# Two column tiles of the last stage made side by side

## The chip, the cores and the metric

The kernel runs on one core of a Trainium2 chip. The metric is device time in microseconds (us) of one execution. Its engines run side by side and meet only through waits: TensorE (PE, with PEld for its weight loads), VectorE (DVE), ScalarE (ACT), GpSimd (POOL) and SyncE (SP), which issues every DMA of the last stage. Each engine takes its instructions strictly in the order in which the program lists them, so that an instruction that waits holds back all that stand behind it on its engine.

## The reference

One layer of a diffusion backbone over 2048 latent tokens and 256 context tokens, width 1024. What matters here is its end, cut down:

```python
b0 = pool_o * silu(pieces[1])
b1 = diff_o * silu(pieces[5])
b2 = gqa_o * silu(pieces[9])
g0, g1, g2 = split(sigmoid(pieces[10]), 3)
y = g0 * (b0 @ w_branch[0]) + g1 * (b1 @ w_branch[1]) + g2 * (b2 @ w_branch[2])
x_new = x + gate * (y @ w_out)
```

`b0`, `b1` and `b2` are 2048 x 512, `w_branch` is three times 512 x 1024, `w_out` 1024 x 1024.

## The kernel before

Before the last stage come the projections, the attention and the gates; none of that is touched. The last stage works on four chunks of 512 tokens, held transposed (128 channels on partitions, 512 tokens in the free dimension). For each chunk it makes eight tiles of `y` (`merge`, phase "m", called m0 to m7 below) and then eight tiles of the output (`finish`, phase "o", called o0 to o7). The 64 steps stand in the list `seq`, in this order, and `n` is a step's place in it.

Products are made in three passes. Each float32 operand is split into a rounded high part and the rest, its low part (`split`: ACT writes the high part, then DVE subtracts it from the source to get the low part), and a product is high x high, high x low, low x high (`PASSES`). A tile of the output is thus 8 tiles of `y` (index k) x 3 passes = 24 matmuls 128x128 by 128x512. Its first two need only the high part of the weights `wt`, the third needs the low part.

What each step of `finish` issues: after k = 3 the split of the `y` tile that was merged last (`late`, set by m7 and therefore only there in o0), the split of the next step's weights (`w_split(n + 1)`), the load of the weights of step n + 3 (`w_load`, 512 KB for an output tile), and the load of the next step's piece of x (`x_load`, the tile `res`); at the end DVE multiplies the sum by the gate and adds x (L1237), and the tile is written out. There are two buffers for raw weights (`wr`) and two for split weights (`wt`): a split of weights can start when the step two before it has done its last matmul, and a load of raw weights when the split of the step two before it is done.

Beside this run the parts of the next chunk's branches: twelve generators (pool g0 to g3, diff h0 to h3, gqa h0 to h3, called p, d and g below), of which `tick`, called once at the head of every step, starts one and takes every active one a stage further. A diff part first issues three loads (L1064: `oD`, `rD`, `sgD`), a tick later multiplies on DVE (L1157, name `b`) and on POOL (L1159, name `b1g`), and a tick later splits the result into `bt` (L1056 on ACT, L1057 on DVE). A pool part makes its `pl` on POOL and DVE (L1131), splits it, and a tick later multiplies it on PE (L1145, `mix`), then on DVE (L1147), and splits it into `bt`. During o0 of the first three chunks the tick starts d1, lets d0 multiply, and lets p3 make `pl`; at o1 it starts d2, lets d1 multiply, and splits p3 and d0; at o2 it starts d3, lets d2 multiply, and splits d1. The last chunk has no parts to make.

All of this is issued in the order in which the Python code is run, on every engine: no scheduler moves it.

Of the kernel before, what the change touches and what calls it, by code (L numbers as in the profile page):

```python
# [16 lines left out]
ALU = mybir.AluOpType  # L17
# [4 lines left out]
P = 128  # L22
D = 1024
KT = D // P
# [14 lines left out]
CH = 512  # L39
# [18 lines left out]
def block_kernel(ctx: ExitStack, tc, x, xT, ctxt, cc, ada_w, ada_bT, norm_gT, w_qkv, w_gate, gains,  # L58
                 rope_row, rope_col, lam, sublnT, pool_w, pool_scaleT, pool_edge, w_br, w_out, out,
                 dbg=None, stop=9):  # L60
    nc = tc.nc
    dma = nc.sync.dma_start
# [26 lines left out]
    gateT = cst.tile([P, KT], F32, name="gateT")  # L89
# [8 lines left out]
    def dump():  # L98
        if dbg:
            for nm, t in (("kD0", kD[0]), ("kD4", kD[4]), ("qD1", qD[1]), ("qD5", qD[5]), ("vD", vD), ("gvD", gvD),  # L100
                          ("oD1", oD[1]), ("oD5", oD[5]), ("uD1", uD[1]), ("sgD1", sgD[1]),
                          ("tD3", tD[3]), ("msD1", msD[1]), ("rD1", rD[1])):
                if nm in dbg:
                    dma(out=dbg[nm], in_=t)
# [12 lines left out]
    def s8(name, shape, dt):  # L117
        return shp.tile(shape, dt, name=name, tag="s8", bufs=8)

    def raw(name):  # L120
        return shp.tile([P, 512], F32, name=name, tag="raw", bufs=4)
# [90 lines left out]
    with tc.tile_pool(name="p1", bufs=1) as sp, tc.tile_pool(name="p1s", bufs=1, space=PSUM) as pp:  # L212
# [242 lines left out]
        wraws, weights, wundo, weps = {}, {}, {}, {}  # L455

        def w_load(kind, k):
            off, width = QKV_CHUNKS[kind]
            wr = sp.tile([P, 512], F32, name="wraw", tag="wraw", bufs=8)
            dma(out=wr[:, :width], in_=w_qkv[k * P:(k + 1) * P, off:off + width])  # L460
            wraws.setdefault(kind, []).append(wr)
# [211 lines left out]
        for n, kind in enumerate(QKV_ORDER):  # L673
# [9 lines left out]
            for t in range(first, NT):  # L683
# [34 lines left out]
                if gating and u < 10:  # L718

                    for m in (2 * u - 4, 2 * u - 3):  # L720
                        if 0 <= m:
                            part, wr = gacc[:, (m % 2) * 512:(m % 2 + 1) * 512], ada_raws.pop(0)
                            if m < 2:
                                nc.vector.tensor_scalar(out=part, in0=wr, scalar1=cct[:, 0, 0:1], scalar2=None,
                                                        op0=ALU.mult)
                            else:
                                nc.vector.scalar_tensor_tensor(out=part, in0=wr, scalar=cct[:, m // 2, 0:1], in1=part,
                                                               op0=ALU.mult, op1=ALU.add)
# [36 lines left out]
    with tc.tile_pool(name="p2", bufs=1) as sp, tc.tile_pool(name="p2s", bufs=1, space=PSUM) as pp:  # L765
# [4 lines left out]
        for n in range(32):  # L770
            for o in range(2):
                rows += [("d", n // 8, n % 8, o, c) for c in range(2)]
                m = 2 * n + o
# [233 lines left out]
        for i in range(NR + 7):  # L1007
# [8 lines left out]
            if i < NR:  # L1016
                kind, h, j, o, c = rows[i]
# [31 lines left out]
    with tc.tile_pool(name="p3", bufs=1) as sp, tc.tile_pool(name="p3s", bufs=1, space=PSUM) as pp:  # L1049
        def acc3(name):  # L1050
            return pp.tile([P, CH], F32, name=name, tag="acc3", bufs=5)

        PASSES = ((0, 0), (0, 1), (1, 0))

        def split(dst, src):
            nc.scalar.activation(out=dst[0], in_=src, func=AF.Copy)  # L1056
            nc.vector.tensor_tensor(out=dst[1], in0=src, in1=dst[0].bitcast(F32), op=ALU.subtract)  # L1057

        def work(name):
            return sp.tile([P, CH], F32, name=name, tag="wk", bufs=6)  # L1060

        def load(src, name="ld"):
            t = sp.tile([P, CH], F32, name=name, tag="ld", bufs=8)
            dma(out=t, in_=src)  # L1064
            return t
# [3 lines left out]
        raws, weights, extras = [], [], []  # L1069
# [9 lines left out]
        def w_split(n):  # L1079
            if n < len(seq):  # L1080
                wr, nk = raws.pop(0)
                wt = sp.tile([P, 2, 12, P], F32R, name="wt3", tag="wt3", bufs=2)
                split((wt[:, 0, :nk], wt[:, 1, :nk]), wr[:, :nk])
                weights.append(wt)

        def x_load(n):
            if n < len(seq):
                ph, c, j = seq[n]
                if ph == "m":
                    extras.append([load(tD[c][8 * br + j]) for br in range(3)])  # L1090
                else:
                    r = raw("res")
                    dma(out=r, in_=xT[j * P:(j + 1) * P, c * CH:(c + 1) * CH])
                    extras.append(r)


        def branch_tile(c, br, k):

            if (c, br) not in bts:
                if (3 * c + br) % 4 == 3:  # L1100
                    bts[c, br] = [s8("bt", [P, 2, 2, CH], F32R) for _ in range(2)]
                else:
                    t = sp.tile([P, 4, 2, CH], F32R, name="bt", tag="bt", bufs=3)
                    bts[c, br] = [t[:, 0:2], t[:, 2:4]]
            return bts[c, br][k // 2][:, k % 2]
# [70 lines left out]
        def tick(new=()):  # L1176

            for p in list(active):
                if next(p, "end") == "end":
                    active.remove(p)  # L1180
            for p in new:
                next(p)
                active.append(p)

        ys = {}

        def y_split(c, j, t):
            if j % 2 == 0:
                ys[c, j // 2] = s8("y", [P, 2, 2, CH], F32R)
            y = ys[c, j // 2][:, j % 2]  # L1190
            split((y[:, 0], y[:, 1]), t)

        def merge(n, c, j):
            nonlocal late
            wb, tg = weights.pop(0), extras.pop(0)
            t = []
            for br in range(3):
                ps = acc3("br")
                m = 0
                for k in range(4):  # L1200
                    for a, b in PASSES:
                        nc.tensor.matmul(ps, lhsT=wb[:, a, 4 * br + k, :], rhs=branch_tile(c, br, k)[:, b],  # L1202
                                         start=(m == 0), stop=(m == 11))
                        m += 1
                w = work("yb")
                nc.vector.scalar_tensor_tensor(out=w, in0=tg[br], scalar=1.0, in1=ps, op0=ALU.add, op1=ALU.mult)  # L1206
                t.append(w)
                if br == 0:
                    if late:
                        y_split(*late)  # L1210
                        late = None
                    w_split(n + 1)
                    w_load(n + 3)
                    x_load(n + 1)
                if br == 1:
                    nc.gpsimd.tensor_tensor(out=t[0], in0=t[0], in1=t[1], op=ALU.add)
            nc.gpsimd.tensor_tensor(out=t[0], in0=t[0], in1=t[2], op=ALU.add)
            late = (c, j, t[0])

        def finish(n, c, j):  # L1220
            nonlocal late
            wo, r = weights.pop(0), extras.pop(0)
            ps = acc3("out")
            m = 0
            for k in range(KT):
                if k == 4:
                    if late:
                        y_split(*late)
                        late = None
                    w_split(n + 1)  # L1230
                    w_load(n + 3)
                    x_load(n + 1)
                for a, b in PASSES:
                    nc.tensor.matmul(ps, lhsT=wo[:, a, k, :], rhs=ys[c, k // 2][:, k % 2, b, :], start=(m == 0),  # L1234
                                     stop=(m == 3 * KT - 1))
                    m += 1
            nc.vector.scalar_tensor_tensor(out=r, in0=ps, scalar=gateT[:, j:j + 1], in1=r, op0=ALU.mult, op1=ALU.add)  # L1237
            dma(out=out[j * P:(j + 1) * P, c * CH:(c + 1) * CH], in_=r)

        pse = sp.tile([P, 4, 16], F32, name="pse")  # L1240
        dma(out=pse, in_=pool_edge)
        psc = sp.tile([P, 4], F32, name="psc")
# [11 lines left out]
        def parts(c):  # L1254
            return [pool_part(c, g) for g in range(4)] + [diff_part(c, h) for h in range(4)] + \
                [gqa_part(c, h) for h in range(4)]

        late = None
# [21 lines left out]
        for n, (ph, c, j) in enumerate(seq):  # L1280
            if ph == "m" and j == 0:
                coming = parts(c + 1) if c + 1 < NCH else []
            if coming and not (ph == "m" and j < 3):
                tick([coming.pop(0)])
            else:
                tick()
            (merge if ph == "m" else finish)(n, c, j)
    dump()


# [67 lines left out]
```

## Time and profile before

| | us |
|---|---|
| median of three runs | 2870.18 (2863.91 to 2872.3) |
| profiled execution, its own time | 2865.6 |
| its span, first to last instruction | 2863.8 |
| PE busy | 2723.5 (95%) |
| DVE, ACT, POOL busy | 2231.2, 1622.5, 699.9 |
| granted TensorE clock, mean | 0.990 of full speed |

The table says that PE is busy nearly all the time. What an edit in the last stage is worth is therefore read from the stretches in which PE stands still there, and from what ended each of them. In the rows below a line of the timeline gives the start, the length, the engine, the line of the kernel, the operation, what it writes and reads, and how often; in square brackets stand the time for which its engine was idle before it and what ended that.

### The profile page before, as it was taken

How to read it: one execution, taken by the hardware profiler on the slowest of the kernel's cores; microseconds unless marked ns; L12 is line 12 of the kernel's file. 1: busy time of each engine (PE TensorE's matmuls, PEld its weight loads, DVE VectorE, ACT ScalarE, POOL GpSimd, SP SyncE). 2: the span in 40 equal slices, each digit the busy share in tenths (PEclk: the TensorE clock that was granted, in tenths of full speed). 3: DMA queues.
4: the chain of work that ended last, by engine and by line, in shares of the span. 5: the costliest groups of instructions: out<-in, count | busy, mean ns of one | idle time of the engine just before them, and what ended most of it. 6: DMA issues, size and time to landing. Idle time of an engine off the chain costs nothing. (4 is left out here: it accounts for less than half of the span.)

```text
span 2863.8 us, 41067 instructions
## 1 busy us (share of the span) xinstructions
PE 2723.5 (95%) x15007; PEld 1590.1 (56%) x15007; DVE 2231.2 (78%) x2845; ACT 1622.5 (57%) x2166; POOL 699.9 (24%) x699
## 2 busy tenths in 40 slices
PE   7999999999999989999989999999999988999999
PEld 2544446545554445455545555555555546787787
DVE  4447687598888898889889999899998846766753
ACT  3844432367666666767757777667777742322221
POOL 1036655311111102010202111112111114443431
PEclk8999999999999999999999999999999999999999
DMA  6345562498978888889898999898998967767674
GB/s 241 129 122 145 152 174 68 106 193 173 185 163 171 183 182 167 172 175 179 173 202 185 187 187 188 178 203 180 186 187 172 179 163 235 250 220 257 211 246 146
DMA packets 1134267, 516.46 MB, mean 180 GB/s; under 512 B 985041, under 2 KB 1038705, under 8 KB 1134065
## 3 DMA queue, kind: packets, MB, share of 16 engines
q1 hardware_dynamic: 1134064, 513.84, 76.3%
q8 instruction: 118, 1.93, 0.3%
q14 instruction: 85, 0.69, 0.1%
HBM read 208.24 MB, written 78.97 MB: 100 GB/s over the span
## 5 line engine op out<-in xcount | busy, mean ns | idle before, releaser
L179 PE MATMUL gate<-hT,gws 128*128 128x512 f16 x3840 | 870.9, 380 | 0.0
L179 PEld LDWEIGHTS <-gws 128*128 128x128 f16 x3840 | 368.4, 98 | 431.0 <-issue 31.8
L829 ACT ACTIVATE pt<-sa,nm,escale 128x1024 f32<-128x1024 f32 x256 | 308.2, 1204 | 428.6 <-DVE nm L826 388.9
L821 PEld LDWEIGHTS <-qt 128*128 128x128 f16 x2560 | 249.8, 98 | 378.0 <-issue 97.4
L532 PE MATMUL qkv<-wt,hT 128*128 128x512 f16 (+1 forms) x1920 | 391.8, 359 | 0.0
L825 DVE TENSOR_REDUCE nm<-sb 128x1 f32<-128x1280 f32 x256 | 379.2, 1481 | 1.5 <-PE sb L821 1.5
L830 ACT ACTIVATE pt<-sb,nm,escale 128x1280 f32<-128x1280 f32 x256 | 360.3, 1407 | 0.0
L824 DVE TENSOR_REDUCE nm<-sa 128x1 f32<-128x1024 f32 x256 | 310.9, 1215 | 51.1 <-PE sa L821 50.8
L912 DVE SCALAR_TENSOR_TENSOR lo<-pt,nm,hi 128x2304 f16<-128x2304 f32 x128 | 337.7, 2639 | 7.5 <-ACT hi L907 4.7
L821 PE MATMUL sb<-kt,qt 128*128 128x512 f16 (+1 forms) x1536 | 320.3, 345 | 24.3 <-ACT pt L830 24.2
L907 ACT ACTIVATE hi<-pt,nm 128x2304 f16<-128x2304 f32 x128 | 283.3, 2213 | 93.3 <-issue 47.0
L821 PE MATMUL sa<-kt,qt 128*128 128x512 f16 x1024 | 262.6, 379 | 34.5 <-ACT pt L829 28.9
L532 PEld LDWEIGHTS <-hT 128*128 128x128 f16 x1920 | 188.3, 98 | 165.7
L1202 PE MATMUL br<-bt,wt 128*128 128x512 f32 x1152 | 267.7, 393 | 1.6 <-DVE wt L1057 1.6
L1202 PEld LDWEIGHTS br<-bt,wt 128*128 128x128 f32 x1152 | 217.2, 189 | 50.7 <-DVE wt L1057 2.7
L936 POOL TENSOR_TENSOR o<-ot 128x256 f32<-128x256 f32 x32 | 20.9, 652 | 837.6 <-ACT ot L932 707.2
L163 POOL TENSOR_SCALAR gws<-gw 128x512 f16<-128x512 f32 x74 | 71.4, 965 | 601.7 <-PE gate L179 597.8
L926 PE MATMUL av<-th,vt 128*128 128x256 f16 x1728 | 198.9, 273 | 0.0
L1234 PE MATMUL out<-y,wt 128*128 128x512 f32 x768 | 185.0, 399 | 11.5 <-DVE wt L1057 4.8
L926 PEld LDWEIGHTS <-vt 128*128 128x128 f16 x1728 | 169.1, 98 | 19.7
L1234 PEld LDWEIGHTS out<-y,wt 128*128 128x128 f32 x768 | 144.9, 189 | 50.7 <-DVE wt L1057 6.6
L888 DVE SCALAR_TENSOR_TENSOR lo<-pt,nm,hi 128x2304 f16<-128x2304 f32 x64 | 167.9, 2624 | 0.4 <-ACT hi L883 0.3
(213 smaller groups left out, 3220.2 us busy)
## 6 DMA issues: line engine op xcount, KB each, us to landing
tD<-gt SPq DMA_DIRECT2D x96, 256.0 KB
wr<-in_w_br SPq DMA_DIRECT2D x32, 768.0 KB
ld<-tD SPq DMA_DIRECT2D x96, 256.0 KB
scan<-in_w_gate SPq DMA_DIRECT2D x40, 512.0 KB
gw<-in_w_gate SPq DMA_DIRECT2D x80, 256.0 KB
qt<-qD SPq DMA_DIRECT2D x256, 64.0 KB
wr<-in_w_out SPq DMA_DIRECT2D x32, 512.0 KB
sgD<-gt SPq DMA_DIRECT2D x48, 256.0 KB
```

The costliest lines, as they stand in the source:

```text
L179: nc.tensor.matmul(ps, lhsT=w[:, b, k, :], rhs=hT[k][:, a, c * CH:(c + 1) * CH], start=(n == 0), stop=(n == 3 * KT - 1))
L532: nc.tensor.matmul(ps[:, :width], lhsT=tokens_of(t, k, a), rhs=wt[k][:, b, :width], start=(n == 0), stop=(n == 3 * KT - 1))
L821: nc.tensor.matmul(dst, lhsT=qt[:, s, o * P:(o + 1) * P], rhs=kt[:, k0:k1], start=(s == 0), stop=(s == 1))
L824: nc.vector.tensor_reduce(out=nm[:, 0:1], in_=sa, axis=AX.X, op=ALU.max, negate=True)
L825: nc.vector.tensor_reduce(out=nm[:, 1:2], in_=sb, axis=AX.X, op=ALU.max, negate=True)
L829: nc.scalar.activation(out=pt[:, :SA], in_=sa, func=AF.Exp, scale=escale[:, m:m + 1], bias=nm[:, 0:1], accum_out=nm[:, 2:3])
L830: nc.scalar.activation(out=pt[:, SA:], in_=sb, func=AF.Exp, scale=escale[:, m:m + 1], bias=nm[:, 0:1], accum_out=nm[:, 3:4])
L907: nc.scalar.activation(out=box["hi"], in_=pt, func=AF.Copy, scale=nm[:, 3:4])
L912: nc.vector.scalar_tensor_tensor(out=lo, in0=pt, scalar=nm[:, 3:4], in1=box["hi"], op0=ALU.mult, op1=ALU.subtract)
L926: nc.tensor.matmul(ps[:, :256], lhsT=vt[:, k, v, :], rhs=pts[a][:, k, :], start=(n == 0), stop=(n == 3 * NKT - 1))
L1202: nc.tensor.matmul(ps, lhsT=wb[:, a, 4 * br + k, :], rhs=branch_tile(c, br, k)[:, b], start=(m == 0), stop=(m == 11))
L1234: nc.tensor.matmul(ps, lhsT=wo[:, a, k, :], rhs=ys[c, k // 2][:, k % 2, b, :], start=(m == 0), stop=(m == 3 * KT - 1))
```

## The change

`finish_two` makes o0 and o1 of a chunk together, in two accumulators. It issues the split of o1's weights first, then the 21 matmuls of o0 with k = 0 to 6, the split of the late `y` tile, the load of step n + 3's weights, the 21 matmuls of o1 with k = 0 to 6, and then the three of o0 and the three of o1 with k = 7, which need the late `y` tile. Between these two threes stand the split of o2's weights, the load of step n + 4's weights and the load of o2's `res`. Both tiles are scaled and written at the end. The loop calls `tick` at o1 as before, and does nothing else there.

```diff
+        def finish_two(n, c):
+            nonlocal late
+            wos, res, pss = [weights.pop(0)], [extras.pop(0)], [acc3("out"), acc3("out")]
+            def products(j, ks):
+                for k in ks:
+                    for m, (a, b) in enumerate(PASSES):
+                        nc.tensor.matmul(pss[j], lhsT=wos[j][:, a, k, :], rhs=ys[c, k // 2][:, k % 2, b, :],
+                                         start=(k == 0 and m == 0), stop=(k == KT - 1 and m == 2))
+            w_split(n + 1)
+            x_load(n + 1)
+            products(0, range(KT - 1))
+            y_split(*late)
+            late = None
+            wos.append(weights.pop(0))
+            res.append(extras.pop(0))
+            w_load(n + 3)
+            products(1, range(KT - 1))
+            products(0, [KT - 1])
+            w_split(n + 2)
+            w_load(n + 4)
+            x_load(n + 2)
+            products(1, [KT - 1])
+            for j in range(2):
+                nc.vector.scalar_tensor_tensor(out=res[j], in0=pss[j], scalar=gateT[:, j:j + 1], in1=res[j],
+                                               op0=ALU.mult, op1=ALU.add)
+                dma(out=out[j * P:(j + 1) * P, c * CH:(c + 1) * CH], in_=res[j])
...
-            (merge if ph == "m" else finish)(n, c, j)
+            if ph == "m":
+                merge(n, c, j)
+            elif j == 0:
+                finish_two(n, c)
+            elif j > 1:
+                finish(n, c, j)
```

On ACT, at the first chunk's o0 to o3, these instructions stood before (wt_23592, wt_23647 and wt_23693 are the weights of o1, o2 and o3; bt<-b1g is the split of a diff part, d0 and then d1):

```order
L1056 ACTIVATE pl_23562<-pl 128x512
L1056 ACTIVATE y<-yb 128x512
L1056 ACTIVATE wt_23592<-wr_23426 128x1024
L1056 ACTIVATE bt<-b_23617 128x512
L1056 ACTIVATE bt<-b1g 128x512
L1056 ACTIVATE wt_23647<-wr_23516 128x1024
L1056 ACTIVATE bt<-b1g 128x512
L1056 ACTIVATE wt_23693<-wr_23595 128x1024
```

And now, in the same place (wt_23579, wt_23633 and wt_23693 are those of o1, o2 and o3):

```order
L1056 ACTIVATE pl_23562<-pl 128x512
L1056 ACTIVATE wt_23579<-wr_23426 128x1024
L1056 ACTIVATE y<-yb 128x512
L1056 ACTIVATE wt_23633<-wr_23516 128x1024
L1056 ACTIVATE bt<-b_23651 128x512
L1056 ACTIVATE bt<-b1g 128x512 x2
L1056 ACTIVATE wt_23693<-wr_23607 128x1024
```

The weights of o1 moved ahead of the late `y`, those of o2 ahead of the splits of p3 and d0, and both diff parts now stand together ahead of the weights of o3.

On DVE, from the late `y` to the weights of o3 (names as above; L1157 writes d1 and then d2), before:

```order
L1057 TENSOR_TENSOR y<-yb,y 128x512
L1057 TENSOR_TENSOR wt_23592<-wr_23426,wt_23592 128x1024
L1237 SCALAR_TENSOR_TENSOR res<-out,gateT,res 128x512
L1147 SCALAR_TENSOR_TENSOR b_23617<-mix,psc,ld 128x512
L1057 TENSOR_TENSOR bt<-b_23617,bt 128x512
L1057 TENSOR_TENSOR bt<-b1g,bt 128x512
L1157 SCALAR_TENSOR_TENSOR b_23624<-ld,sbl 128x512
L1057 TENSOR_TENSOR wt_23647<-wr_23516,wt_23647 128x1024
L1237 SCALAR_TENSOR_TENSOR res<-out,gateT,res 128x512
L1057 TENSOR_TENSOR bt<-b1g,bt 128x512
L1157 SCALAR_TENSOR_TENSOR b_23670<-ld,sbl 128x512
L1057 TENSOR_TENSOR wt_23693<-wr_23595,wt_23693 128x1024
```

And now:

```order
L1057 TENSOR_TENSOR wt_23579<-wr_23426,wt_23579 128x1024
L1057 TENSOR_TENSOR y<-yb,y 128x512
L1057 TENSOR_TENSOR wt_23633<-wr_23516,wt_23633 128x1024
L1266 SCALAR_TENSOR_TENSOR res<-out,gateT,res 128x512 x2
L1147 SCALAR_TENSOR_TENSOR b_23651<-mix,psc,ld 128x512
L1057 TENSOR_TENSOR bt<-b_23651,bt 128x512
L1057 TENSOR_TENSOR bt<-b1g,bt 128x512
L1157 SCALAR_TENSOR_TENSOR b_23658<-ld,sbl 128x512
L1057 TENSOR_TENSOR bt<-b1g,bt 128x512
L1157 SCALAR_TENSOR_TENSOR b_23670<-ld,sbl 128x512
L1057 TENSOR_TENSOR wt_23693<-wr_23607,wt_23693 128x1024
```

The scaling of o0 moved from ahead of the diff parts to behind the weights of o2, beside that of o1; everything from L1147 on stands behind both, and no step of the output lies between the work of the tick at o1 and that of the tick at o2.

On SP, in the same place (wr_23607 and wr_23636 are the raw weights of o3 and o4, before wr_23595 and wr_23650; the loads from oD_89 and rD_101 are those of d2):

```order
-L1076 DMA wr_23595<-in_w_out 128x1024
-L1093 DMA res<-in_xT 128x512
-L1238 DMA out_dram<-res 128x512
+L1093 DMA res<-in_xT 128x512
+L1076 DMA wr_23607<-in_w_out 128x1024
+L1076 DMA wr_23636<-in_w_out 128x1024
+L1093 DMA res<-in_xT 128x512
+L1268 DMA out_dram<-res 128x512 x2
 L1064 DMA ld<-oD_89 128x512
 L1064 DMA ld<-rD_101 128x512
```

The loads of d2 now stand behind the raw weights of o4 and behind both output tiles.

## Rows read from the trace of the kernel before

**Rows 1.** The page's first line: the span of the profiled execution

```profile
span 2863.8 us, 41067 instructions
```

**Rows 2.** Groups of instructions of the last stage: busy, mean ns, idle before, releasers

```profile
L1234 PE MATMUL out<-y,wt 128*128 128x512 f32 x768 | 185.0, 399 | 11.5 <-DVE wt L1057 4.8 <-ACT y L1056 3.8 <-DVE y L1057 2.9
```

**Rows 3.** Timeline of PE, first chunk, from o0's third matmul to o1

```profile
2460.14 4.71 PE L1234 MATMUL out<-y,wt 128*128 128x512 f32 x19 [1.56 <-DVE wt L1057]
...
2465.97 0.49 PE L1234 MATMUL out<-y,wt 128*128 128x512 f32 x1 [1.12 <-ACT y L1056]
...
2467.44 1.00 PE L1234 MATMUL out<-y,wt 128*128 128x512 f32 x2 [0.98 <-DVE y L1057]
...
2468.24 1.48 PE L1145 MATMUL mix<-pl,pw 128*128 128x512 f32 x3
...
2469.52 8.84 PE L1234 MATMUL out<-y,wt 128*128 128x512 f32 x34
```

**Rows 4.** Timeline of DVE, ACT and POOL, first chunk, at the late y

```profile
2465.30 0.61 ACT L1056 ACTIVATE y<-yb 128x512 fp32r<-128x512 f32 x1
...
2465.82 1.04 ACT L1056 ACTIVATE wt<-wr 128x1024 fp32r<-128x1024 f32 x1
...
2466.04 0.75 DVE L1157 SCALAR_TENSOR_TENSOR b<-ld,sbl 128x512 f32<-128x512 f32 x1
2466.70 0.68 DVE L1057 TENSOR_TENSOR y<-yb,y 128x512 fp32r<-128x512 f32 x1
2466.86 1.65 POOL L1159 TENSOR_TENSOR b1g<-b,ld 128x512 f32<-128x512 f32 x1 [3.36 <-DVE b L1157]
2467.30 2.29 DVE L1057 TENSOR_TENSOR wt<-wr,wt 128x1024 fp32r<-128x1024 f32 x1
```

**Rows 5.** Timeline, last chunk: PE's whole output phase, and ACT's split for o2

```profile
2814.66 44.96 PE L1234 MATMUL out<-y,wt 128*128 128x512 f32 x192
...
2820.45 1.06 ACT L1056 ACTIVATE wt<-wr 128x1024 fp32r<-128x1024 f32 x1 [1.86 <-PE out L1234]
```

**Rows 6.** Timeline, first three chunks: end of o1, late y, and o1 in the third

```profile
2476.06 0.75 DVE L1237 SCALAR_TENSOR_TENSOR res<-out,gateT,res 128x512 f32<-128x512 f32 x1 [1.36 <-PE out L1234]
...
2584.51 0.61 ACT L1056 ACTIVATE y<-yb 128x512 fp32r<-128x512 f32 x1
...
2595.25 0.75 DVE L1237 SCALAR_TENSOR_TENSOR res<-out,gateT,res 128x512 f32<-128x512 f32 x1 [1.33 <-PE out L1234]
...
2705.38 0.61 ACT L1056 ACTIVATE y<-yb 128x512 fp32r<-128x512 f32 x1
...
2709.74 6.56 PE L1234 MATMUL out<-y,wt 128*128 128x512 f32 x27 [0.34 <-DVE wt L1057]
```

**Rows 7.** Timeline, first chunk, from o0's scaling to the split of o3's weights

```profile
2469.52 0.74 DVE L1237 SCALAR_TENSOR_TENSOR res<-out,gateT,res 128x512 f32<-128x512 f32 x1
...
2472.50 0.42 SPq L1064 DMA_DIRECT2D ld<-rD  x1
...
2476.42 1.05 ACT L1056 ACTIVATE wt<-wr 128x1024 fp32r<-128x1024 f32 x1
...
2477.71 0.46 SPq L1064 DMA_DIRECT2D ld<-rD  x1
2478.04 0.75 DVE L1157 SCALAR_TENSOR_TENSOR b<-ld,sbl 128x512 f32<-128x512 f32 x1 [0.63 <-DMA ld<-rD]
...
2478.71 1.22 DVE L1057 TENSOR_TENSOR wt<-wr,wt 128x1024 fp32r<-128x1024 f32 x1
```

**Rows 8.** Stretches of three chunks: busy (x) by engine, granted clock, DMA share, GB/s

```profile
2467.40:2469.60 2.20, 2.16 (x6) 1.69 (x7) 2.20 (x2) 0.00 (x0) 1.11 (x1) 0.57 0.03 13
2584.00:2588.50 4.50, 2.40 (x8) 1.68 (x8) 3.87 (x4) 2.07 (x3) 1.66 (x1) 0.85 0.46 173
2704.70:2709.80 5.10, 2.44 (x9) 1.48 (x9) 4.32 (x6) 2.10 (x3) 1.67 (x1) 1.00 0.39 148
```

## The prediction, made before the changed kernel ran

> **What bounds the kernel now.** I read the groups of instructions of the last stage first, then the timeline around o0 of each chunk, then the stretches with their granted clock. PE is the engine that sets the end, so the question is only where PE stands still in the output phase. The group of its 768 matmuls says 11.5 us in all, by three releasers: the low part of weights 4.8, and the late `y`, high part 3.8 and low part 2.9 [rows 2]. That is the whole stock, 0.4% of the span of 2863.8 us [rows 1], and only the 6.7 us of `y` are what the change is aimed at.
>
> The timeline shows where they lie. In the first chunk PE waits 1.56 us for o0's own low weights, does 19 matmuls, waits 1.12 for the high `y`, does one, waits 0.98 for the low `y` [rows 3]. The second and third chunk repeat the pattern. In the last chunk PE runs all 192 matmuls without a gap [rows 5]: no parts of a next chunk are made there, and DVE and ACT are in time. So at most three places can gain, and a fourth can only lose. The pitch of a matmul is (44.96 - 0.39)/191 = 0.233 us [rows 5], with 0.39 for the last one's own length (the mean is 399 ns [rows 2]); a tile of 24 takes 5.60, three take 0.70, two take 0.47.
>
> **Step 1, the late y is needed later.** Now 42 matmuls of k = 0 to 6 come before it instead of 21. The wait for `y` goes. What is late next is the weights of o1, which are now wanted after 21 matmuls. In the first chunk these end at 2460.14 + 19 x 0.233 = 2464.57 [rows 3]. The split of o1's weights takes the place of `y` on ACT and DVE, so ACT starts it when it started `y`, at 2465.30 [rows 4]; it takes 1.04 [rows 4], and PE follows an operand by 0.06 (the low `y` was ready at 2466.70 + 0.68 = 2467.38, PE went on at 2467.44) [rows 3, 4]. PE goes on at 2466.40, does two matmuls until 2466.87, and then needs the low part. DVE starts that where it started `y`, at 2466.70.
>
> How long it takes is the first choice. The same instruction took 2.29 us at 2467.30, with POOL's multiplication running until 2468.51 [rows 4], and 1.22 with none at its start [rows 7]. In rows 4 the DVE subtraction that began 0.16 us ahead of POOL's took its plain 0.68, and the one that began while POOL ran was held. Now the weights stand in that first place, so I take 1.22; the other end is 2.29, or 1.07 more in each of three chunks. The Trainium skill, "SBUF — State Buffer", section "Who interferes with whom", has the same as a rule: a DVE instruction with two inputs in SBUF and a GpSimd instruction that reads SBUF exclude each other, and whichever issues first blocks the other in full. By that rule everything hangs on those 0.16 us; if POOL came first, each of the three chunks would lose the whole rest of the GpSimd instruction; the trace agrees with both halves (0.68 unheld, 2.29 held).
>
> With 1.22 the low part is ready at 2467.92 and PE goes on at 2467.98: 19 matmuls to 2472.41, three of o0 (the late `y` has long been split) to 2473.11, three of o1 to 2473.81, `mix` to 2474.51.
>
> **Step 2, the weights of o2.** Their buffer is free only when o0's last matmul is done, 0.19 us after the next one starts (the last chunk's o1 starts at 2814.66 + 5.60 = 2820.26, ACT at 2820.45) [rows 5]. So ACT starts at 2473.11 + 0.19 = 2473.30 and ends at 2474.34; the high part is in time. DVE ends 1.22 + 0.06 later, at 2475.62, and PE has o2's third matmul at 2475.68, which is 0.70 later than without the wait. It is 10.38 after ACT's start at 2465.30.
>
> In the kernel before, o1 ended 0.19 before DVE's scaling at 2476.06 [rows 6], so o2's third matmul was at 2475.87 + 0.47 = 2476.34. The change gains 0.66 in the first chunk. The second by the same offset: 2584.51 + 10.38 = 2594.89 against 2595.25 - 0.19 + 0.47 = 2595.53, gain 0.64. The third: 2705.38 + 10.38 = 2715.76 against 2709.74 + 22 x 0.233 + 0.47 = 2715.34, loss 0.42 [rows 6]. So of 6.7 us of waits hardly 0.9 is left: new waits for weights take their place. In the last chunk, which had no waits, only step 2 remains, without `mix` to cover it: o2's third matmul could come 0.70 + 0.47 = 1.17 after o0's last has made room; its low part comes 0.19 + 1.06 + 0.06 + 1.22 + 0.06 = 2.59 after. Loss 1.42.
>
> **Step 3, the weights of o3.** This is where I expect the time to go. All that the ticks at o1 and o2 issue now stands behind both scalings, and only one tile, o2, is left to cover it. On ACT the weights of o3 stand behind d1's split; on DVE also behind d2's multiplication, which waits for d2's loads; on SP those loads stand behind the raw weights of o4 (which wait for the split of o2) and both output tiles.
>
> The way by ACT: in the kernel before, 2476.42 - 2469.52 = 6.90 us passed from o0's scaling to ACT's start on o3 [rows 7]. Now the scaling starts when o2's low weights are done, about 2475.60, and there are two: 2475.60 + 0.67 + 6.90 = 2483.17, and the high part is ready at 2484.27. If nothing holds POOL's multiplication on the way (1.22 of DVE's weights lay in it before) this can be some 0.8 less.
>
> The way by the loads: d2's `rD` load was issued 2477.71 - 2476.06 = 1.65 after a scaling [rows 6, 7]; now 2475.60 + 0.67 + 1.65 = 2477.92. It took 2478.04 - 2472.50 = 5.54 to land and release DVE [rows 7], so 2483.46. DVE then multiplies (0.67 to its next start, 2478.71 - 2478.04), subtracts (1.22), and PE follows: 2485.41 for o3's third matmul. Without a wait it would be at 2475.68 + 5.60 = 2481.28. The stall is 4.1 us, in each of the first three chunks. Bounds: by ACT and DVE alone, with POOL unheld and the loads in time, 3.1; with a landing 1.1 slower, since more is queued ahead (the raw weights and two output tiles), 5.2. A gain is excluded: nothing in this chain is removed. I take 4.1, the row's own.
>
> Further on nothing is late: o4's weights stand behind d2's split and d3, with a whole tile of 5.6 us, which covered them before. Accumulators do not bind (five), nor does the end: the last tile is made as before.
>
> **Step 4, the clock.** The granted clock fell behind the waits of the first two chunks (0.57 and 0.85 in these stretches) and not behind those of the third (1.00), whose waits are no shorter [rows 8]; it moves between 2.4 GHz and 1.2 GHz. In the first chunk the three `mix` matmuls took 2469.52 - 2468.24 = 1.28 instead of 0.70, and o1 2475.87 - 2469.52 = 6.35 instead of 5.60: 1.3 us for one fall [rows 3, 6]. My times of after hold none, so each that comes is to be added, at six places now (before o2 and in o3). From zero to six, 0 to 8 us; I take two, as before, 2.7 us. The Trainium skill, "TensorE: Matmul & The Clock Gate", Part 1, says that an array that has been idle is put to half its clock and that the moment varies from run to run; by that rule the long wait in o3 would be the surest place, three falls and 4 us; rows 8 agree that equal waits need not give equal falls.
>
> **The sum.** 3 x 4.1 + 1.42 - 0.66 - 0.64 + 0.42 + 2.7 = 15.5 us. The profiled execution took 2865.6, its span 2863.8 and the 1.8 around it unchanged, so 2881.1; against the median of 2870.18, 2885.7. I predict 2886.
>
> **Rivals.**
> - *Loads and clock at their upper ends*: stalls of 5.2, five falls of the clock. 15.6 + 0.5 + 6.5 = 22.6, 2893. For it: more bytes stand ahead of d2's loads than before, and there are twice as many waits. Against it: the DMA queues are nearly empty until o4's raw weights are issued. Chance 0.2.
> - *POOL first in step 1*: 1.07 more in three chunks. o3's stall hangs on the same chain and moves with it, so 15.5 + 3.2 = 18.7, 2889. Chance 0.1.
> - *No new wait in o3, not slower*: the parts of d1 and d2 get done beside o2, and o3's weights are ready. Then -0.9 + 1.4, and with no fall of the clock 2870.7; with PE's waits fewer it might even reach a few us below. It decides if o3's low part is ready at 2481.2, which asks that 6.9 us of ACT, DVE and POOL work shrink to under 4 and that the loads land in 1.5. For it: DVE is free of one weight split in between. Against it: every row of a load in these stretches takes over 5 us. Chance 0.12.
>
> **How the numbers follow.** The forecast has 0.58. The first two rivals are slower too, so slower has about 0.83 (a little of the forecast's lower end, 3 x 3.1 with no fall, is 9.8 us and near the line), same 0.14, faster 0.03. A measurement of this kernel can tell about 0.3%, 8.6 us, from no change. Lower end of the range: 9.8 us less a few of the runs' scatter, 2874; upper end from the first rival with the same allowance, 2895.
>
> **What would show it.** Right: in the changed profile the `y` waits of PE are gone; PE waits about 1.8 and 1.1 us for ACT and DVE `wt` in o1; the third matmul of o2 follows a short wait; and in o3 PE waits first for ACT `wt`, then for DVE `wt`, together about 4 us in three chunks, while DVE's L1157 waits for `rD`. The last chunk shows about 1.4 us of waits in o2 where there were none. Wrong: if o3 starts without a wait, step 3 falls and with it the forecast; if waits for `y` remain, step 1 does.

## The result, and the profile after

The changed kernel took 2899.29 us (median of five runs, 2897.58 to 2900.7) against 2869.89 for the kernel before; the ratio is 1.0107, with an interval of 1.0094 to 1.012. Predicted were 2886 and a range up to 2895: the direction was right, the size little more than half of it. One execution of e4 and one of e7 below that took 7931 and 4431 us are left out of all ratios. The profiled execution took 2898.57, its span 33.0 us more than before.

How much of this is the change is read from one stretch: from o0's third matmul to the first matmul of the next chunk's merge. Ahead of it the executions differ by some us from run to run: in this one 2.85, o0's third matmul being at 2462.99 instead of 2460.14 [rows 3]. The three merge phases in between take the same time in both, to 0.01 us. In the first chunk the stretch is 2520.75 - 2462.99 = 57.76 us, before 2509.46 - 2460.14 = 49.32. The second and third give 58.93 and 59.30 against 49.30 and 48.76, and the output phase of the last chunk 46.47 against 44.96. Together 8.4 + 9.6 + 10.5 + 1.5 = 30.1 us, which is the measured difference of 29.4 within the scatter.

The groups of PE's matmuls in the last stage answer to [rows 2] (count, busy and mean ns, idle before, releasers):

```profile
L1234 PE MATMUL out<-y,wt 128*128 128x512 f32 x576 | 145.3, 412 | 17.2 <-DVE wt L1057 10.0 <-ACT wt L1056 7.2
...
L1248 PE MATMUL out<-y,wt 128*128 128x512 f32 x192 | 53.5, 435 | 11.6 <-DVE wt L1057 6.6 <-ACT wt L1056 5.0
```

The `y` waits are gone, as meant. In their place PE waits for weights alone, 28.8 us instead of 11.5 in all: 17.3 more. And the same 768 matmuls are busy for 198.8 us instead of 185.0: 13.8 more. So nearly half of the loss is not waiting at all. The timeline of PE over the first chunk's first four tiles (start, length, line, count, idle before) answers to [rows 3]:

```profile
2462.99 4.71 PE L1248 MATMUL out<-y,wt 128*128 128x512 f32 x19 [1.39 <-DVE wt L1057]
2469.25 0.74 PE L1248 MATMUL out<-y,wt 128*128 128x512 f32 x2 [1.55 <-ACT wt L1056]
2470.83 7.63 PE L1248 MATMUL out<-y,wt 128*128 128x512 f32 x25 [0.84 <-DVE wt L1057]
2478.30 0.85 PE L1145 MATMUL mix<-pl,pw 128*128 128x512 f32 x3
2478.99 0.71 PE L1234 MATMUL out<-y,wt 128*128 128x512 f32 x2
2480.22 5.40 PE L1234 MATMUL out<-y,wt 128*128 128x512 f32 x22 [0.52 <-DVE wt L1057]
2487.88 0.73 PE L1234 MATMUL out<-y,wt 128*128 128x512 f32 x2 [2.25 <-ACT wt L1056]
2491.11 29.80 PE L1234 MATMUL out<-y,wt 128*128 128x512 f32 x118 [2.51 <-DVE wt L1057]
```

The same two runs of matmuls, behind o1's and behind o3's weights, in the second and the third chunk:

```profile
2598.47 7.40 PE L1248 MATMUL out<-y,wt 128*128 128x512 f32 x25 [0.84 <-DVE wt L1057]
...
2619.20 30.53 PE L1234 MATMUL out<-y,wt 128*128 128x512 f32 x118 [2.71 <-DVE wt L1057]
...
2728.97 8.57 PE L1248 MATMUL out<-y,wt 128*128 128x512 f32 x25 [0.55 <-DVE wt L1057]
...
2750.34 29.87 PE L1234 MATMUL out<-y,wt 128*128 128x512 f32 x118 [2.65 <-DVE wt L1057]
```

Every wait that steps 1 to 3 named is there: o1's weights (1.55 and 0.84), o2's low part (0.52), o3's high and low part (2.25 and 2.51). But at the pitch of 0.233 us the 25 matmuls behind o1's wait would take 5.99 us and take 7.63, and the 118 behind o3's would take 27.5 to the next chunk's first matmul and take 29.64. The stretches (busy by engine with counts, then granted clock, DMA share, GB/s) say why:

```profile
2470.80:2478.40 7.60, 7.57 (x26) 6.03 (x27) 1.66 (x1) 0.55 (x1) 1.11 (x1) 0.78 0.26 81
2480.20:2485.40 5.20, 5.18 (x22) 4.06 (x22) 3.90 (x6) 1.16 (x2) 0.46 (x1) 1.00 0.82 225
2485.40:2491.10 5.70, 0.95 (x3) 0.30 (x2) 2.62 (x4) 1.58 (x2) 1.31 (x2) 0.79 0.93 294
2491.10:2496.00 4.90, 4.89 (x12) 3.84 (x13) 3.11 (x4) 1.58 (x2) 2.71 (x2) 0.55 0.75 232
...
2619.20:2625.00 5.80, 5.79 (x14) 4.54 (x15) 3.10 (x4) 1.93 (x3) 3.23 (x2) 0.50 0.80 248
```

Behind both waits PE is busy all the time at a granted clock of 0.78 (behind o1), 0.55 (behind o3) and 0.50 (behind o3 in the second chunk): in the first chunk's o3 it does 12 matmuls in 4.9 us where 21 would fit. The rows answer to [rows 8]; there a fall lay partly over waits, here it lies over work.

### The profile page after: what moved, and what is told of

It reads as the page before. It is cut to its first block, busy times and chain, and to the rows that moved or that the text cites. A ratio compares the mean times of both kernels' runs of the same rounds, so it can differ in the third digit from the quotient of the medians.

```text
span 2896.8 us, 41069 instructions
## 1 busy us (share of the span) xinstructions
PE 2736.9 (94%) x15007; PEld 1597.8 (55%) x15007; DVE 2233.6 (77%) x2845; ACT 1623.5 (56%) x2166; POOL 696.9 (24%) x699
## 5 line engine op out<-in xcount | busy, mean ns | idle before, releaser
L879 DVE SCALAR_TENSOR_TENSOR pt<-pt,nm 128x2304 f32<-128x2304 f32 x64 | 168.3, 2629 | 0.0
L1234 PE MATMUL out<-y,wt 128*128 128x512 f32 x576 | 145.3, 412 | 17.2 <-DVE wt L1057 10.0
```

## The experiments

All ratios are to the kernel before, from runs on the same chip. The column of stretches is the sum over the first three chunks, from o0's third matmul to the next merge, in the profiled execution of each; the last column is the output phase of the last chunk. e7 is the changed kernel once more; of it only the ratio is given.

| | ratio to before (95%) | three stretches, us | last chunk, us |
|---|---|---|---|
| before | 1 | 147.4 | 45.0 |
| changed | 1.0107 (1.0094 to 1.012) | 176.0 | 46.5 |
| e7, changed again | 1.0098 (1.0084 to 1.0113) | | |
| e1, tick between the tiles | 1.001 (1.0001 to 1.0019) | 148.6 | 46.5 |
| e2, ticks in a row alone | 1.0049 (1.0035 to 1.0063) | 162.1 | 45.0 |
| e3, waits filled | 1.0063 (1.0049 to 1.0077) | 163.9 | 46.5 |
| e4, k = 7 earlier | 1.0072 (1.0058 to 1.0086) | 165.6 | 45.0 |
| e5, d2's loads earlier | 1.0076 (1.0062 to 1.009) | 166.3 | 46.5 |
| e6, edits together | 1.001 (1.0001 to 1.0019) | 150.0 | 45.1 |
| e8, weights ahead everywhere | 0.9957 (0.9943 to 0.997) | 138.4 | 45.1 |
| e9, weights ahead alone | 1.0012 (1.0004 to 1.0021) | 151.6 | 45.0 |

### e1 and e2: the two ticks in a row

e1 undoes one part of the change: it puts the tick of o1 back between the tiles.

```diff
+        def next_parts(ph, j):
+            if coming and not (ph == "m" and j < 3):
+                tick([coming.pop(0)])
+            else:
+                tick()
...
             y_split(*late)
             late = None
+            next_parts("o", 1)
...
-            if coming and not (ph == "m" and j < 3):
-                tick([coming.pop(0)])
-            else:
-                tick()
+            if not (ph == "o" and j == 1):
+                next_parts(ph, j)
```

> The tick of o1 is issued between the two tiles (behind the split of the late y, ahead of o1's products) instead of behind both, so that the ticks of o1 and o2 are a tile apart again; all else as in the changed kernel. Theory A (the two ticks in a row make o3's weights late, and the wait also pulls the granted clock down behind it): the wait of about 4.8 us in o3 and the fall of the clock behind it (about 2.3) go in three chunks, 3 x 7.1 = 21 us less than the changed kernel's 2899, so about 2878; the waits for o1's weights stay, with their fall of the clock. Theory B (what costs is the split of o2's weights, which now must wait for o0's last three matmuls): those stand where they stood, so within 4 us of 2899.

Measured: 1.001, 25 to 28 us below the changed kernel's two ratios, where 21 were expected. PE in the first chunk:

```profile
2474.08 6.09 PE L1254 MATMUL out<-y,wt 128*128 128x512 f32 x25 [0.60 <-DVE wt L1057]
2480.67 0.74 PE L1234 MATMUL out<-y,wt 128*128 128x512 f32 x2 [0.50 <-ACT wt L1056]
2481.93 33.42 PE L1234 MATMUL out<-y,wt 128*128 128x512 f32 x142 [0.52 <-DVE wt L1057]
```

The wait in o3 is gone: 142 matmuls run on from o2's third (in the third chunk PE waits 1.13 once more, for o4's low weights). The 25 take 6.09, and 6.09 and 6.10 in the other chunks, so the fall behind o1 is gone too; that is the gain beyond the expected one. `mix` now fills part of the wait for o1's weights, which may be why, but that is not shown: in e4 and e5 below the fall behind o1 stays away in two chunks of three with nothing in the wait. Theory B (o2's weights) falls: their two short waits are still there, and cost little.

e2 puts the ticks in a row into the kernel before, and leaves all else.

```diff
...
+            if not (ph == "o" and j == 1):
+                next_parts(ph, j)
+            if ph == "o" and j == 2:
+                next_parts(ph, j)
...
```

> The kernel before, with its two tiles one after the other, and only the tick of o1 held back until just before that of o2. Theory A: in o3 PE now waits for weights that stand behind both diff parts and d2's loads; by the rows of before the low part is ready at about 2485.2 against 2481.9, 3.3 us, and with a fall of the clock of about 2 behind it 5.3 in each of three chunks: about 2886, 16 over before's 2870. Theory B: nothing about the weights has changed, so within 4 us of 2870.

Measured: 1.0049, 12 us by the medians (14 by the ratio) where 16 were expected. PE in o1 and in o3 of the first chunk:

```profile
2479.03 8.10 PE L1234 MATMUL out<-y,wt 128*128 128x512 f32 x22 [1.03 <-DVE wt L1057]
...
2494.34 0.73 PE L1234 MATMUL out<-y,wt 128*128 128x512 f32 x2 [0.93 <-ACT wt L1056]
2495.92 27.79 PE L1234 MATMUL out<-y,wt 128*128 128x512 f32 x118 [0.85 <-DVE wt L1057]
```

The wait arises without any tile side by side, but it is 0.93 and 0.85, not 2.25 and 2.51, and the clock falls behind it in one chunk of three (29.3 us for these 118 instead of 27.8). That is some 8 of the 14.7 us that its three stretches gain; the rest lies in o1, where `mix` no longer stands between the tiles and PE waits 1.03, 0.34 and 1.04 us for o1's weights; there the clock falls too, and the 22 matmuls behind take 8.10, 6.05 and 8.12 us in the three chunks, where 5.3 would do. So two ticks in a row do make o3 late by themselves; what else the change moves makes that wait twice as long and more.

### e3: what the clock costs

```diff
+        def fill(c, times):
+            if c + 1 < NCH:
+                ps = acc("fill")
+                for _ in range(times):
+                    nc.tensor.matmul(ps, lhsT=pw[:, 0, 0, :], rhs=ys[c, 0][:, 0, 0, :], start=True, stop=True)
...
```

It is called with 7 and 4 in o1, and with 10 and 10 in o3, ahead of the first and the third matmul.

> The changed kernel, with matmuls that nobody reads put into PE's waits of the first three chunks: 7 ahead of o1's first matmul, 4 ahead of its third, 10 ahead of o3's first, 10 ahead of its third (0.233 us each, so 1.6, 0.9, 2.3, 2.3 us where PE stood still 1.8, 1.1, 2.5, 2.7). The waits themselves end as before. Theory A, clock part: the granted clock stays at 1.00 behind them, the 25 matmuls that took 7.4 to 8.6 us take 5.8, and those after o3's wait run at 0.233 each; 3 x (2.0 + 2.4) = 13 us less, about 2886. Theory C (the lost time beyond the waits has another cause, such as operands or accumulators that come late without being shown): the same matmuls are as slow as before, 2899 or a little more.

Measured: 1.0063, 10 to 13 us below the changed kernel's two ratios, and 12.1 by the stretches; 13 were expected. The same matmuls as above, behind the filled waits:

```profile
2476.50 5.75 PE L1258 MATMUL out<-y,wt 128*128 128x512 f32 x24
...
2495.23 27.80 PE L1238 MATMUL out<-y,wt 128*128 128x512 f32 x118 [0.48 <-DVE wt L1057]
```

```profile
2476.50:2482.10 5.60, 5.60 (x26) 4.53 (x25) 1.30 (x1) 0.46 (x1) 0.75 (x1) 1.00 0.36 102
2495.20:2501.00 5.80, 5.77 (x25) 4.69 (x26) 3.46 (x5) 1.87 (x3) 3.29 (x2) 1.00 0.85 252
```

With matmuls in the waits whose result nobody reads, the clock stays at 1.00 and the work behind runs at its pitch, in all three chunks. From o1's third matmul to o2's and from o3's third to the next chunk that is 12.3 us less. The waits ended nearly as before: from o0's third matmul to o1's to 0.02 us in the first two chunks, and from o2's to o3's 0.3 later, 1.0 earlier and the same in the three. In the third chunk o1's third comes 0.9 later, because the clock fell one wait sooner, behind o0's own weights, which nothing filled (1.79 us; 19 matmuls took 6.25 instead of 4.70). So some 12 us of the 29 are the clock's, shown by taking them away; theory C falls.

### e4 and e5: what makes the wait in o3

```diff
-            products(1, range(KT - 1))
+            products(1, range(4))
             products(0, [KT - 1])
...
-            products(1, [KT - 1])
+            products(1, range(4, KT))
```

> The changed kernel, with the three matmuls of o0 for k = 7 (and with them the split of o2's weights) moved up from behind 21 to behind 12 of o1's matmuls. Theory A: the short wait of o2 (0.5 and 0.2 us) goes, also in the last chunk (1.4 us there); the scaling of o1, and with it the work of the ticks and d2's loads, comes about 2.2 us earlier because it no longer stands behind the low part of o2's weights, so o3's third matmul comes 2.2 us earlier: 3 x 2.2 + 1.4 = 8 us less, about 2891, with the waits in o3 still 3 to 4 us. Theory B (o2's weights are the cause): most of the loss goes, 2880 or below.

Measured: 1.0072, 7 to 10 us less than changed, as theory A had it; the last chunk gets its 1.5 us back. By the stretches it is more, 10.4 and these 1.5, but 3.8 of it is two falls of the clock behind o1 that did not come here, though the wait in o1 is the same as in the changed kernel. PE from o2 on:

```profile
2483.89 5.76 PE L1234 MATMUL out<-y,wt 128*128 128x512 f32 x24
2490.68 0.73 PE L1234 MATMUL out<-y,wt 128*128 128x512 f32 x2 [1.03 <-ACT wt L1056]
2494.09 29.19 PE L1234 MATMUL out<-y,wt 128*128 128x512 f32 x118 [2.68 <-DVE wt L1057]
```

o2 runs without a wait, and o3 waits 1.03 for ACT instead of 2.25; for DVE it waits 2.68, 3.17 and 2.69 in the three chunks, no less than the 2.51, 2.71 and 2.65 of the changed kernel.

In e5 the loads of d2 are issued inside `finish_two`, and the tick at o1 then takes d2 over without starting a part of its own:

```diff
...
+            if coming:
+                early.append(coming.pop(0))
+                next(early[0])
             w_load(n + 3)
...
+            if ph == "o" and j == 1:
+                tick()
+                active.extend(early)
+                early.clear()
...
```

> The changed kernel, with only the three loads of d2 issued earlier, ahead of the raw weights of o3 and o4; the work of both ticks stays where it was. If the wait in o3 has two parts (weights behind d1's split on ACT, then behind d2's multiplication on DVE, which waits for its loads), only DVE's wait for the loads goes, 1.6 to 2.3 us in three chunks: 6 us less than the changed kernel's 2899, with PE still waiting 2.2 us for ACT in o3 and about 1 for DVE behind it, and the clock still falling. If the loads alone make o3 late, the wait in o3 goes altogether and its fall of the clock with it: 20 us less.

Measured: 1.0076, 6 to 9 us less than changed, where 6 were expected. PE in o3:

```profile
2496.78 1.22 PE L1234 MATMUL out<-y,wt 128*128 128x512 f32 x2 [2.26 <-ACT wt L1056]
2498.36 30.05 PE L1234 MATMUL out<-y,wt 128*128 128x512 f32 x118 [0.36 <-DVE wt L1057]
```

The wait for the low part falls from 2.51 to 0.36, the one for the high part stays, and the clock still falls in all three chunks (29.9 us to the next chunk instead of 27.5). From o2's third matmul to o3's the three chunks take 5.8 us less; the other 3.9 by which the stretches shrink are falls behind o1 that did not come in two chunks, with the wait there unchanged. So the wait in o3 has both parts that step 3 named: ACT's, behind d1's split, and DVE's, behind d2's loads.

### e6, e8 and e9: a version that gains

e6 puts the tick between the tiles, moves k = 7 of o0 up behind 15 matmuls of o1, scales o0 at once, and issues the split of the next weights ahead of the tick at o0 and o2.

```diff
...
+            if ph == "o" and j in (0, 2):
+                w_split(n + 1)
...
+            products(1, range(5))
             products(0, [KT - 1])
             w_split(n + 2)
+            scaled(0)
+            next_parts("o", 1)
...
+            products(1, range(5, KT))
+            scaled(1)
```

> All that the runs so far point to in one kernel: two tiles side by side; the split of the next weights ahead of the tick at o0 and o2; o0's three matmuls for k = 7 behind 15 of o1's; then the split of o2's weights, o0's scaling and only then the tick of o1. By theory A no wait for weights or y over 1 us is left in o0 to o3 behind o0's third matmul, the clock does not fall, and from that matmul to the next chunk's first is about 46 us instead of 49.1 before: 3 x 3.2 = 10 us less than the kernel before, about 2860. If the waits only move on to another tile, or the parts come late for the next chunk, it is within 3 us of before or slower.

Measured: 1.001, not the 10 us gain.

```profile
2480.67 12.17 PE L1235 MATMUL out<-y,wt 128*128 128x512 f32 x50
2494.98 22.20 PE L1235 MATMUL out<-y,wt 128*128 128x512 f32 x94 [2.14 <-DVE wt L1057]
```

And DVE ahead of o4's low weights:

```profile
2493.04 0.75 DVE L1157 SCALAR_TENSOR_TENSOR b<-ld,sbl 128x512 f32<-128x512 f32 x1 [1.73 <-DMA ld<-rD]
```

o0 to o3 run as hoped in the first two chunks (o2's third matmul 12.3 us after o0's in the first, before 16.2; in the third the clock falls behind o0's own weights), but PE now gets ahead of the parts, and the wait turns up in o4: its low weights stood on DVE behind d3's multiplication, which waited 1.73 us for its loads. e8 therefore issues the split ahead of the tick at every output step.

```diff
-                    if j != 2:
-                        w_split(n + 1)
...
-            if ph == "o" and j in (0, 2):
+            if ph == "o" and j != 1:
                 w_split(n + 1)
```

> The kernel before this one in the study (all edits together), with the split of the next weights ahead of the tick at every output step, not at o0 and o2 alone. There PE waited 2.1 to 3.5 us for o4's low weights, which stood on DVE behind d3's multiplication and its loads; with the split ahead of the tick nothing waits for d3's loads but the parts. Expected: no wait over 1 us behind o0's third matmul, 46 us from there to the next chunk's first, 10 us less than the kernel before's, so about 0.4% faster. If the wait moves on again (the parts come late for the next chunk's merge, or the scalings wait for res), no faster than before.

Measured: 0.9957 (0.9943 to 0.997), 2862.72 against 2873.39 us: faster than the kernel before, by the 10 us expected, and so than the changed one.

```profile
2465.16 9.16 PE L1253 MATMUL out<-y,wt 128*128 128x512 f32 x37 [1.31 <-DVE wt L1057]
2474.16 0.85 PE L1145 MATMUL mix<-pl,pw 128*128 128x512 f32 x3
2474.85 2.26 PE L1253 MATMUL out<-y,wt 128*128 128x512 f32 x9
2476.95 34.11 PE L1233 MATMUL out<-y,wt 128*128 128x512 f32 x144
```

From o0's third matmul PE does not stand still until the next chunk's merge, in the first and the second chunk; in the third it waits 0.41 for `y`. What remains is the 1.3 to 1.8 us for o0's own weights. In the profiled execution the three stretches gain 9.0 us, and 2.1 of them go again in the third chunk's merge, where PE waits 0.52 and 1.19 us for weights and waited 0.30 before; so some 7 of the 10 can be placed there.

e9 is the kernel before with the weights ahead of the tick at every output step and the tiles one after the other.

> The kernel before, one tile after the other, with only the split of the next weights ahead of the tick at every output step. If making the two tiles side by side is worth something once the weights are in time, the waits for the late y stay here (2.1 us and a fall of the clock in the first three chunks) and this kernel is within 3 us of before; if the order of weights and tick is all that matters, it gains as much as the kernel with both, about 10 us.

Measured: 1.0012. The late `y`, now behind one more split, costs more than before:

```profile
2472.89 0.50 PE L1233 MATMUL out<-y,wt 128*128 128x512 f32 x1 [2.26 <-ACT y L1056]
2474.36 0.73 PE L1233 MATMUL out<-y,wt 128*128 128x512 f32 x2 [0.97 <-DVE y L1057]
```

So the order of the weights alone gains nothing (e9), and the two tiles with the tick between them alone gain nothing either (e1, 1.001); together, in e8, they gain 0.4%. That the order must hold at o3 to o7 too is shown by one edit, from e6 (1.001) to e8 (0.9957). e8 also has o0's k = 7 and its scaling moved up, and no run takes these two out again, so what share they have is not shown.

## Why the prediction was wrong, point by point

- **Step 1 and step 2 held.** From o0's third matmul to o2's I had 15.54, 15.54 and 15.94 us in the first three chunks. Measured were 17.23, 16.98 and 18.56; without the excess of the 25 slow matmuls (7.63, 7.40 and 8.57 instead of 5.99) that is 15.59, 15.57 and 15.98. The last chunk lost 1.51, predicted 1.42, and has the two waits in o2 that [rows 5] did not have:

```profile
2857.93 0.73 PE L1234 MATMUL out<-y,wt 128*128 128x512 f32 x2 [0.45 <-ACT wt L1056]
2859.20 33.40 PE L1234 MATMUL out<-y,wt 128*128 128x512 f32 x142 [0.53 <-DVE wt L1057]
```

  The choice of 1.22 for o1's low weights held as well; in rows of DVE and POOL of the changed kernel, answering to [rows 4]:

```profile
2469.55 1.22 DVE L1057 TENSOR_TENSOR wt<-wr,wt 128x1024 fp32r<-128x1024 f32 x1
2469.71 2.20 POOL L1159 TENSOR_TENSOR b1g<-b,ld 128x512 f32<-128x512 f32 x1 [3.36 <-DVE b L1157]
2470.68 1.78 DVE L1057 TENSOR_TENSOR y<-yb,y 128x512 fp32r<-128x512 f32 x1
```

  The weights came 0.16 us ahead and took 1.22; POOL's 2.20 (1.27 at 2484.94, with no DVE work beside it) and the `y`'s 1.78 (0.68 in [rows 4]), each behind the one ahead, were held. The second and the third chunk have 1.22 as well. The Trainium skill, "SBUF — State Buffer", "Who interferes with whom", has this as whoever issues first blocking the other in full; the trace agrees within 0.13 us, since a wait for the whole rest of the other would make them 2.33 and 1.91. So the engines do not meet only through the program's waits, as I wrote ahead of the prediction.
- **Step 3 was right in mechanism and too small in size.** Predicted 4.1 us in each of three chunks, 12.3; o3's third matmul came 5.29, 5.98 and 5.43 later than 5.60 behind o2's, 16.7 in all. The row behind it (scaling, loads, multiplication, weights; it answers to [rows 7]):

```profile
2480.08 1.41 DVE L1266 SCALAR_TENSOR_TENSOR res<-out,gateT,res 128x512 f32<-128x512 f32 x2
...
2482.51 0.95 SPq L1064 DMA_DIRECT2D ld<-rD  x1
...
2486.78 1.04 ACT L1056 ACTIVATE wt<-wr 128x1024 fp32r<-128x1024 f32 x1
...
2489.17 0.75 DVE L1157 SCALAR_TENSOR_TENSOR b<-ld,sbl 128x512 f32<-128x512 f32 x1 [1.57 <-DMA ld<-rD]
2489.84 1.22 DVE L1057 TENSOR_TENSOR wt<-wr,wt 128x1024 fp32r<-128x1024 f32 x1
```

  In the first chunk the load was issued 2.43 after the scaling, as reckoned (2.32), but released DVE 6.66 later, not 5.54; in the third it was the same (2.43 and 6.80). I had that as the upper bound and left it out of the sum. In the second chunk it was the other way round: the load took 5.17, but was issued 4.61 after the scaling, because the two output tiles ahead of it held SP's queue for 3.07 us instead of 0.86:

```profile
2608.49 3.07 SPq L1268 DMA_DIRECT2D out_dram<-res  x2
...
2612.09 0.45 SPq L1064 DMA_DIRECT2D ld<-rD  x1
...
2617.26 0.75 DVE L1157 SCALAR_TENSOR_TENSOR b<-ld,sbl 128x512 f32<-128x512 f32 x1 [2.27 <-DMA ld<-rD]
```

  Two output tiles and o4's raw weights were ahead of the load; that they made it land later is argued, not shown by a run that takes them away alone. The way by ACT was shorter than reckoned, 6.7 from the scaling to ACT's start in all three chunks instead of 0.67 + 6.90, so the loads decided. And the lower bound of 3.1 does not come out of its rows: with 0.8 less the third matmul is at 2483.17 - 0.8 + 1.04 + 0.06 + 1.22 + 0.06 = 2484.75, 3.5 late.
- **Step 4 failed.** I counted two falls of the clock at 1.3 us, 2.7 in all. There were six, one behind o1's and one behind o3's wait in each of three chunks: 1.64 + 1.41 + 2.58 behind o1, and 2.10 + 2.83 + 2.17 behind o3, 12.7 us. e3 takes 12.3 of them away. Two things were wrong in the step. The number: I carried the count of before over to a kernel with twice as many waits. And the price: 1.3, read from a single fall, where these six cost 1.4 to 2.8 each; at 1.3 even six falls would have been only 8 us. The Trainium skill's sentence that I cited ("TensorE: Matmul & The Clock Gate", Part 1: an idle array goes to half clock) pointed to o3 as the surest place. The traces agree: behind o3's wait the clock fell in all nine chunks of the changed kernel, e4 and e5 (0.50 to 0.74 granted), behind o1's in five of the nine (0.68 to 0.81). The sum that I drew from it, three falls and 4 us, I did not take, but it would have closed only 1.3 of the 10.0 us.
- **The sum.** 15.5 predicted, + 10.0 for the clock, + 4.4 for o3, + 0.2 for the rest: 30.1, as measured by the stretches.
- **The rivals.** The first, loads and clock at their upper ends, was nearest: 5.2 per stall came out at 5.6, and five falls were priced 6.5 where six cost 12.7. POOL did not come first. That o3 might not wait is refuted in all three chunks.

Not settled: why the clock falls behind one wait and not behind its like. In e4 the wait in o1 was 1.57 and 0.84 in the first and the second chunk alike; the 25 matmuls behind took 7.65 in the first, 6.10 in the second:

```profile
2475.71 7.65 PE L1248 MATMUL out<-y,wt 128*128 128x512 f32 x25 [0.84 <-DVE wt L1057]
...
2600.84 6.10 PE L1248 MATMUL out<-y,wt 128*128 128x512 f32 x25 [0.84 <-DVE wt L1057]
```

So that all three falls behind o1 came in the changed kernel's profiled execution is in part chance.

## What to carry to other kernels

When steps are merged, ask what was paced by the steps: here a generator of side work was called once per step, and two calls in a row put twice the work in front of the next step's weights on every in-order engine. Price a new wait of the matrix engine as the wait plus a fall of its clock over the work behind it, unless other matmuls can fill it; here a fall cost 1.4 to 2.8 us, and it came behind many of the waits, not behind all. And issue what the critical engine needs next ahead of the side work: with the side work between the two tiles, this kernel was no faster than before while the splits issued at some output steps stood behind it (e6), and 0.4% faster once they stood ahead of it at all output steps (e8).

## What the runs showed of the hardware

A matrix engine that stood still for about 2.3 and 2.6 us, with two matmuls between, behind 5.4 us of work ran at 0.50 to 0.59 of full speed in the stretch of about 5 us behind (changed kernel, three chunks of three), which is its lower level of 1.2 GHz for most of it; with 10 matmuls that nobody reads in each wait it stayed at 2.4 GHz. Unexpected at the prediction was the size: 12.7 us for six such falls, nearly twice all the waits for `y` that the change set out to remove (6.7 us).
